# One of the weight sums of a Strassen product moves from VectorE to GpSimd

## The chip, the cores and the metric

The kernel runs on one core of one Trainium2 chip. The metric is the device time of one execution in microseconds (us). Before the change it is 801.15 us, the median of three runs (801.14, 801.15 and 801.73).

The core's engines are named as in its profile: PE is TensorE (matrix products; PEld is its load of the stationary operand, which overlaps the products), DVE is VectorE, ACT is ScalarE, POOL is GpSimd, and SP is the engine whose queue issues most DMAs. Every engine works through its own queue in order. "PEq", "SPq" and the like are the sequencers, which issue DMAs and carry out waits.

## The reference

One block of a decoder on 512 tokens of 1024 values, in float32: a mixer (a state-space part with 16 heads and a pooling part, with one input and one output projection), a cross-attention into 256 memory tokens, and a SwiGLU layer of width 2816. Each is preceded by an RMS norm and added to the residual. A last RMS norm gives the output. The change is in the SwiGLU layer alone:

```python
def swiglu(u, w_gate_up, w_down):
    gate, up = jnp.split(u @ w_gate_up, 2, axis=-1)
    return (jax.nn.silu(gate) * up) @ w_down

h = h + swiglu(rmsnorm(h, ffn_norm[l]), w_gate_up[l], w_down[l])
return rmsnorm(h, final_norm)
```

## The kernel before

**Precision.** Products run on TensorE in a rounded format (float32r). To reach float32 precision, every operand is split in two: `hi` is the operand rounded by ScalarE (a cast), `lo` is the remainder, operand minus `hi`, taken by VectorE. A product is then three matmuls: hi by hi, hi by lo, lo by hi. For activations the parts are called t_xh and t_xl (or t_xq where both lie in one tile), for weights `whi` and `wlo`. The cast of a weight tile is line 202, its remainder line 204; both handle 128 x 1024 elements, the unit in which weights are loaded.

**Seven products in place of eight.** The two matrix products of SwiGLU use Strassen's scheme in Winograd's form: operands are cut into 2 x 2 quadrants, and seven products of sums of quadrants replace eight products of quadrants. For the weights, with quadrants 11, 12, 21 and 22, the products are numbered by "form":

- forms 1, 2 and 4 are the quadrants 11, 12 and 22 themselves;
- form 5 is 21 + 22 and form 7 is 21 + 11;
- form 6 is form 5 + quadrant 11;
- form 3 is form 6 + quadrant 12.

The sums of the activations are made on chip by `forms` (lines 1126 to 1163), for one pair of activation tiles at a time: VectorE adds and subtracts (lines 1141, 1142, 1149, 1151), ScalarE casts (line 1132), and VectorE takes the remainders (line 1136).

**The stages.** The layer is cut into 17 chunks of weights: ten "g" chunks of 128 x 1024 (gate and up, blocks 0 to 4, two chunks each), one "g" chunk for block 5, and six "d" chunks (down, three blocks of two; the last of these is 512 wide). The order is a list written out by hand, SPEC: blocks g0 and g1, then d0, then g2 and g3, d1, g4 and g5, d2. Within a block the forms run in the order 1, 2, 5, 6, 3, 7, 4. In a d block, the products of forms 1, 2 and 5 are given in pieces, as the activations that they need come out of two turns (`i_turnff`, a transposition on TensorE, copies on ScalarE, and then `forms`) that stand beside the first of them. PSUM banks are named gA, gB, gC and dA, dB, dC after the output that they gather: forms 1, 6, 7 and 4 go to A, 5 and 3 to B, 2 to C. VectorE drains the banks (lines 1066, 1095 and 1211) and notes the last of these drains in `st["drained"]`.

**How the weight sums are made.** `load_strassen` (lines 147 to 173) loads quadrants by DMAs from SP's queue. For forms 5 and 7 it loads quadrant 21 and then adds the other quadrant by an accumulating DMA, which is issued from GpSimd's queue (line 171). `split_unit` (lines 182 to 211) is a generator of three steps, the sum if there is one, the cast and the remainder. When it has split form 2, it issues the sum for form 6 as another accumulating DMA from GpSimd's queue: form 5 is added onto the tile of quadrant 11 (line 210, "wq<-raw" in the profile). Only block g5 makes form 6 on VectorE (line 189). For form 3 it adds form 6 to the tile of quadrant 12, in place, on VectorE (line 193). The next step of the generator is the cast that reads the sum.

**What sets the order.** The program gives the order in which instructions are written; `advance` (end of the program) runs `split_unit` for the weights of the coming slot, and loads up to seven weight units ahead. A planner of the framework then places the instructions on each engine's queue by that priority and by its own estimate of when their operands are there. `after(later, earlier)` adds an edge which has no wait at run time, since both instructions are on one engine, and which makes the planner keep that order. The add of line 193 has such an edge behind the drain which was the latest when form 5 of the same chunk was split (lines 194, 195 and 201).

**Buffers.** There are six tiles for raw weights, two each for quadrants 11 and 12 of a chunk ("wq" in the profile), four for `whi`, five for `wlo`, and six PSUM banks for these products.

Of the kernel before, what the change touches and what calls it, by code (L numbers as in the profile page):

```python
# [10 lines left out]
ALU = mybir.AluOpType  # L11
# [49 lines left out]
def hybrid_block(ctx: ExitStack, tc: tile.TileContext, a: dict, out: bass.AP,  # L61
                 act_bufs=69, la=1, wb=(6, 4, 5), eng="", dact=(0, 1), raw_n=6, warm=12, spec=None, start=START, smm=START_MM, hu=1, dbg=None):
    nc = tc.nc
# [11 lines left out]
    def nm(base):  # L75
        uid[0] += 1
        return f"{base}_{uid[0]}"
# [69 lines left out]
    def load_strassen(key):  # L147

        _, c, f = key
        n = units[key][1]  # L150

        def quad(q):
            return a["w_s"][c, QUAD[q], :, :n]

        def plain(q, tag=None):
            if tag:
                t = act.tile([P, NC, 2, P], F32, tag=tag, name=nm("wq"), bufs=2).rearrange("p c q l -> p (c q l)")
            else:
                t = wraw.tile([P, 1024], F32, tag="raw", name=nm("raw"))
            nc.sync.dma_start(t[:, :n], quad(q))  # L160
            return t

        if f == 1:
            sw[c, 1] = plain("11", "m")
        elif f == 2:
            sw[c, 2] = plain("12", "m2")
        elif f == 4:
            sw[c, 4] = plain("22")
        elif f == 7 or f == 5 and (c, 5) not in sw:
            sw[c, f] = plain("21")  # L170
            nc.gpsimd.dma_start(sw[c, f][:, :n], quad("11" if f == 7 else "22"), accum_op=ALU.add)  # L171
        ready[key] = None
# [9 lines left out]
    def split_unit(key):  # L182
        n = units[key][1]
        raw = ready[key]
        if key[0] == "s":
            c, f = key[1:]
            if f == 6 and (c, 6) not in sw:
                sw[c, 6] = sw.pop((c, 1))
                nc.vector.tensor_tensor(out=sw[c, 6][:, :n], in0=sw[c, 6][:, :n], in1=sw[c, 5][:, :n], op=ALU.add)
                yield  # L190
            if f == 3:
                sw[c, 3] = sw.pop((c, 2))
                add = nc.vector.tensor_tensor(out=sw[c, 3][:, :n], in0=sw[c, 3][:, :n], in1=sw[c, 6][:, :n], op=ALU.add)  # L193
                if sw[c, "drained"] is not None:
                    after(add, sw[c, "drained"])
                yield
            raw = sw[c, f]
        hi = whi_p.tile([P, 1024], F32R, tag="hi", name=nm("whi"))
        lo = wlo_p.tile([P, 1024], F32R, tag="lo", name=nm("wlo"))
        if key[0] == "s" and f == 5:  # L200
            sw[c, "drained"] = st.get("drained")
        nc.scalar.copy(hi[:, :n], raw[:, :n])  # L202
        yield
        nc.vector.tensor_tensor(out=lo[:, :n], in0=raw[:, :n], in1=hi.bitcast(F32)[:, :n], op=ALU.subtract)  # L204
        ready[key] = (hi, lo)
        if key[0] == "s" and f == 2 and CHUNKS[c][:2] != ("g", 5):
            if (c, 5) not in sw:
                load_strassen(("s", c, 5))
            sw[c, 6] = sw.pop((c, 1))
            nc.gpsimd.dma_start(sw[c, 6][:, :n], sw[c, 5][:, :n], accum_op=ALU.add)  # L210
        yield

    def after(later, earlier):
        tc.add_manual_dep(later.ins, earlier.ins.name,
                          mybir.DependencyInfo(mybir.DependencyClass.NoSync, mybir.DependencyReason.DATA),
                          reason="order on one engine")
# [41 lines left out]
    sw = {}  # L258
# [79 lines left out]
    def i_start(its):  # L338
        it = Item(keys=["dt"] + [k for i in its[1:] for k in i.keys])

        def prep():
# [16 lines left out]
            for kind, i in [(t[0], int(t[1])) for t in start.split()]:  # L358
                if kind == "x":
                    st["xg"][i] = split("xg", xt[i], col(V_MIX + i))  # L360
                elif kind == "w":
                    drain(split_unit(it.keys[i]))
                elif kind in "hH":
                    n = units[it.keys[i]][1]
                    if kind == "h":
                        raws[i] = ready[it.keys[i]]
                        ready[it.keys[i]] = (whi_p.tile([P, 1024], F32R, tag="hi", name=nm("whi")),
                                             wlo_p.tile([P, 1024], F32R, tag="lo", name=nm("wlo")))
                    c = slice(0, n // 2) if kind == "h" else slice(n // 2, n)
                    hi, lo = ready[it.keys[i]]  # L370
                    split_into(hi[:, c], lo[:, c], raws[i][:, c])
                elif kind == "q":
                    sq_acc("xacc", xt[i])
                elif kind == "r":
                    drain(rms1.split())
                else:
                    drain(advance(i))
# [931 lines left out]
    def advance(t):  # L1309
        nonlocal lpos, spos  # L1310
        want = need_[min(t, len(slots) - 1)] - lead
        while spos < want:
            while lpos < min(spos + (7 if plan[spos][0] == "s" else wb[0] - 1), len(plan)):
                load_unit(plan[lpos])
                lpos += 1
            yield from split_unit(plan[spos])
            spos += 1
# [145 lines left out]
```

## Time and profile before

| | before |
|---|---|
| median of three runs | 801.15 us |
| profiled execution, its own time | 802.26 us |
| span of the profiled execution | 800.6 us |
| mean granted clock of TensorE | 0.994 |
| TensorE busy | 786.6 us, 98% |
| VectorE busy | 617.7 us, 77% |
| ScalarE busy | 487.5 us, 61% |
| GpSimd busy | 44.7 us, 6% |
| instructions | 10506 |

A row of a group names the line, the engine, the operation, "out<-in" by tiles, the shapes and the count; behind it stand the busy time, the mean duration of one in ns, and the idle time of the engine just before, with what ended it. A row of the waits is "who line <- what it waited for: us in total, times, longest us". A row of the timeline has the start, the duration (of all, where several are merged, "x2"), the engine, the line and the tiles, and in brackets the idle time before it with what ended that. A row of the windows has the stretch, its length, and for each engine the busy time and the count; then the granted clock of TensorE as a share of full speed, the share of the DMA engines, and GB/s. A row of the chain of waits has the start, the length and what the time went to. Instructions of one engine overlap a little: an instruction of 1.22 us on VectorE is followed by the next after 1.14.

### The profile page before, as it was taken

What the parts mean: (1) busy time and instruction counts of PE and PEld (TensorE: products, weight loads), DVE (VectorE), ACT (ScalarE), POOL (GpSimd) and SP (SyncE); (2) the same over time, 40 slices, a digit from 0 to 9 for tenths busy, and PEclk for the clock granted to TensorE, in tenths of its full rate; (3) what the DMA queues carried; (4) which work ended last, traced back from release to release, by engine and by line L of the source; (5) the groups of instructions that cost most, each with busy time, mean ns of one, the idle gap of its engine ahead of it and who ended that gap; (6) DMA issues with size and microseconds to landing.
All of it is one profiled execution on the core that took longest, in us unless ns stands there. A gap on an engine that the chain in (4) does not pass through costs nothing.

```text
span 800.6 us, 10506 instructions
## 1 busy us (share of the span) xinstructions
PE 786.6 (98%) x3856; PEld 662.1 (83%) x3856; DVE 617.7 (77%) x906; ACT 487.5 (61%) x777; POOL 44.7 (6%) x60
## 2 busy tenths in 40 slices
PE   9999999999999999999999999998999999999995
PEld 7878888888888889888888888887888887888984
DVE  7989969999884897346656667878766789767897
ACT  8667699567954456335544695755354666355864
POOL 0000000000000000000000001011111011101000
PEclk9999999999999999999999999999999999999998
DMA  8253425143574225322366278787779797879602
GB/s 329 89 171 106 130 75 178 53 129 102 185 262 142 86 99 179 111 79 80 114 149 158 54 158 229 188 239 155 214 176 266 178 249 164 227 166 269 160 15 105
DMA packets 40131, 124.42 MB, mean 155 GB/s; under 512 B 4736, under 2 KB 7168, under 8 KB 40080
## 3 DMA queue, kind: packets, MB, share of 16 engines
q1 hardware_dynamic: 32880, 98.33, 36.8%
q0 software_dynamic: 7200, 25.43, 17.7%
q8 instruction: 30, 0.49, 0.3%
q14 instruction: 21, 0.17, 0.1%
HBM read 113.48 MB, written 2.13 MB: 144 GB/s over the span
## 4 chain that ended last, share of the span: by engine, by line
PE 85%; DVE 7%; DMA 3%; ACT 3%; issue 2%; SPq 0%; ACTq 0%; DVEq 0%
PE gA L1054 13%; PE gB L1054 8%; PE dA L1054 6%; PE gC L1054 4%; PE dB L1054 3%; PE v L117 3%; PE v L118 3%; PE v L116 2%; DVE wlo L204 2%; PE wo L118 2%; PE op L118 2%; PE op L116 2%; PE wo L116 2%; PE q L117 2%; PE op L117 2%; PE q L116 2%
## 5 line engine op out<-in xcount | busy, mean ns | idle before, releaser
L202 ACT CAST whi<-raw 128x1024 fp32r<-128x1024 f32 (+1 forms) x127 | 131.4, 1040 | 131.1 <-issue 20.4
L204 DVE TENSOR_TENSOR wlo<-raw,whi 128x1024 fp32r<-128x1024 f32 (+1 forms) x127 | 152.3, 1208 | 61.3 <-ACT whi L202 60.7
L202 ACT CAST whi<-wq 128x1024 fp32r<-128x1024 f32 (+1 forms) x68 | 69.2, 1026 | 53.5 <-PE dA L1054 19.8
L204 DVE TENSOR_TENSOR wlo<-wq,whi 128x1024 fp32r<-128x1024 f32 (+1 forms) x68 | 80.4, 1189 | 25.8 <-ACT whi L202 25.6
L1054 PE MATMUL gA<-whi,t_xh 128*128 128x512 f32 (+1 forms) x192 | 71.7, 373 | 0.0
L1054 PE MATMUL gA<-wlo,t_xh 128*128 128x512 f32 (+1 forms) x192 | 71.4, 372 | 0.0
L1054 PE MATMUL gA<-whi,t_xl 128*128 128x512 f32 (+1 forms) x192 | 71.3, 371 | 0.0
L171 POOL DMA_DIRECT2D raw<-w_s x34 | 29.3, 862 | 655.0 <-DVE t_Pl L240 405.6
L1054 PEld LDWEIGHTS gA<-wlo,t_xh 128*128 128x128 f32 x192 | 36.1, 188 | 6.3
L1054 PEld LDWEIGHTS gA<-whi,t_xh 128*128 128x128 f32 x192 | 36.1, 188 | 6.3
L1054 PEld LDWEIGHTS gA<-whi,t_xl 128*128 128x128 f32 x192 | 36.2, 188 | 6.2
L1054 PE MATMUL dA<-whi,t_xl 128*128 128x512 f32 x88 | 34.5, 392 | 3.2 <-DVE t_xl L1136 3.2
L1054 PE MATMUL dA<-wlo,t_xh 128*128 128x512 f32 x88 | 34.3, 390 | 0.0
L1054 PE MATMUL dA<-whi,t_xh 128*128 128x512 f32 x88 | 34.0, 391 | 0.1
L1070 ACT ACTIVATE t_gu<-t_gu,s 128x512 f32<-128x512 f32 (+1 forms) x24 | 16.4, 687 | 27.9 <-DVE t_gu L1066 27.9
L193 DVE TENSOR_TENSOR wq<-wq,wq 128x1024 f32<-128x1024 f32 (+1 forms) x17 | 20.3, 1192 | 14.0 <-DMA wq<-raw 13.9
L1054 PE MATMUL gB<-whi,t_xq 128*128 128x512 f32 (+1 forms) x96 | 27.6, 371 | 0.0
L1132 ACT CAST t_xh<-t_x 128x512 fp32r<-128x512 f32 x30 | 18.6, 620 | 14.1 <-DVE t_x L1142 9.5
L116 PE MATMUL z<-t_uh,whi 128*128 128x512 f32 x64 | 25.2, 394 | 0.6 <-ACT t_uh L232 0.6
L116 PE MATMUL wo<-t_oh,whi 128*128 128x512 f32 x64 | 25.2, 394 | 0.0
L116 PE MATMUL v<-t_uh,whi 128*128 128x512 f32 x64 | 25.1, 392 | 0.0
L116 PE MATMUL q<-t_hgh,whi 128*128 128x512 f32 x64 | 25.1, 392 | 0.0
(382 smaller groups left out, 2237.8 us busy)
## 6 DMA issues: line engine op xcount, KB each, us to landing
raw<-w_u SPq DMA_DIRECT2D x76, 512.0 KB, 3.3
raw<-w_s SPq DMA_DIRECT2D x48, 512.0 KB, 4.3
wq<-w_s SPq DMA_DIRECT2D x32, 512.0 KB, 5.1
raw<-w_s POOLq DMA_DIRECT2D x32, 512.0 KB, 6.8
wq<-raw POOLq DMA_DIRECT2D x15, 512.0 KB, 7.4
t_x<-xT SPq DMA_DIRECT2D x16, 256.0 KB, 5.3
t_abc<-d_acs SPq DMA_DIRECT2D x16, 256.0 KB, 4.5
out<-t_hT SPq DMA_DIRECT2D x8, 256.0 KB, 2.3
```

The source lines that it names most:

```text
L116: nc.tensor.matmul(ps, whi, xhi, start=start, stop=False)
L117: nc.tensor.matmul(ps, whi, xlo, start=False, stop=False)
L118: nc.tensor.matmul(ps, wlo, xhi, start=False, stop=stop)
L171: nc.gpsimd.dma_start(sw[c, f][:, :n], quad("11" if f == 7 else "22"), accum_op=ALU.add)
L193: add = nc.vector.tensor_tensor(out=sw[c, 3][:, :n], in0=sw[c, 3][:, :n], in1=sw[c, 6][:, :n], op=ALU.add)
L202: nc.scalar.copy(hi[:, :n], raw[:, :n])
L204: nc.vector.tensor_tensor(out=lo[:, :n], in0=raw[:, :n], in1=hi.bitcast(F32)[:, :n], op=ALU.subtract)
L1054: nc.tensor.matmul(it.ps[tt], p[:, ts_], w[:, ws], start=first, stop=(c, i, n) == pairs[-1] and p is xh and w is wl, skip_group_check=True)
L1070: st["silu"] = nc.scalar.activation(g, g, AF.Silu, scale=st["r3",][:, c:c + 1])
L1132: nc.scalar.copy(h if w is None else h[:, w], src)
```

## The change

The add of form 3 is written to GpSimd in place of VectorE, with the same operands and in the same place of the program. The edge that kept it behind a drain of PSUM is not made any more; the note of that drain in line 201 stays, unused.

```diff
             if f == 3:
                 sw[c, 3] = sw.pop((c, 2))
-                add = nc.vector.tensor_tensor(out=sw[c, 3][:, :n], in0=sw[c, 3][:, :n], in1=sw[c, 6][:, :n], op=ALU.add)
-                if sw[c, "drained"] is not None:
-                    after(add, sw[c, "drained"])
+                nc.gpsimd.tensor_tensor(out=sw[c, 3][:, :n], in0=sw[c, 3][:, :n], in1=sw[c, 6][:, :n], op=ALU.add)
                 yield
```

There are 17 such adds, one for each chunk. The add of line 189 (form 6 of block g5) stays on VectorE.

## The prediction

> **What bounds the kernel now.** I read the page's busy table first, then who TensorE waits for in the stretch that holds the 17 adds (440 us to the end), then that stretch by windows, and last the chain of waits around the two holes found there.
>
> ```profile
> span 800.6 us, 10506 instructions
> PE 786.6 (98%) x3856; PEld 662.1 (83%) x3856; DVE 617.7 (77%) x906; ACT 487.5 (61%) x777; POOL 44.7 (6%) x60
> ```
> ```profile
> PE dA L1054 <- DVE t_xl L1136: 3.2, 2, 2.0
> ```
> ```profile
> core 0: us, PE busy (x) PEld busy (x) DVE busy (x) ACT busy (x) POOL busy (x), PEclk, DMA share, GB/s
> 552.70:554.80 2.10, 0.09 (x2) 0.07 (x1) 2.10 (x5) 0.62 (x1) 0.00 (x0) 1.00 0.69 217
> 555.80:559.30 3.50, 3.50 (x10) 2.73 (x9) 3.50 (x7) 2.46 (x3) 0.86 (x1) 0.51 0.75 179
> 674.00:676.00 2.00, 0.85 (x4) 0.41 (x3) 2.00 (x6) 0.62 (x1) 0.00 (x0) 1.00 1.02 277
> ```
>
> TensorE is busy 98% of the span, so work taken off VectorE is worth only what TensorE waits for VectorE. Behind the first 440 us that is two holes, 3.2 us in all, both before a dA product that waits for t_xl, a remainder which `forms` makes (L1136). The windows show them: 2.0 us at 552.7, and 1.15 us at 674.5. They also show what the longer one costs afterwards: from 555.8 the granted clock is 0.51 for 3.5 us, which loses 3.5 x 0.49 = 1.7 us. Behind the shorter one it stays at 1.00. So the two holes and the clock together are worth 2.01 + 1.15 + 1.7 = 4.9 us; the changed lines can take no more than that out of TensorE's time.
>
> The chain of waits through the first hole names its cause:
>
> ```profile
> 541.74 6.94 DMA wq<-raw
> ...
> 548.71 0.04 DVE wq L193
> ...
> 549.85 1.29 DVE t_xl L1136 x2
> 551.13 2.27 DVE wlo L204 x2
> ...
> 554.73 1.20 PE dA L1054 x4
> ```
>
> The accumulating DMA that makes form 6 of the second weight chunk lands at 548.7; the add of form 3 (L193), which needs it, stands in VectorE's queue ahead of the splits that TensorE is waiting for.
>
> **The change, part by part.** What it removes from VectorE, from the view of line 193 and from VectorE's waits between 440 and 775 us:
>
> ```profile
> L193 DVE TENSOR_TENSOR wq<-wq,wq x17: 684/1225/1227, 448.6 to 771.3; 128x1024 f32<-128x1024 f32 x16, 128x512 f32<-128x512 f32 x1
> ```
> ```profile
> DVE wq L193 <- DMA wq<-raw: 13.9, 11, 2.3
> ```
>
> That is 16 x 1.225 + 0.68 = 20.3 us of work and 13.9 us of waits for the DMA. Nearly all lies beside TensorE's work and is worth nothing. What counts is the two places. VectorE's timeline around the first, ScalarE's casts and TensorE's rows:
>
> ```profile
> 546.25 0.42 DVE L1151 SCALAR_TENSOR_TENSOR t_x<-t_x,t_fa 128x256 f32<-128x256 f32 x1
> 548.71 1.23 DVE L193 TENSOR_TENSOR wq<-wq,wq 128x1024 f32<-128x1024 f32 x1 [2.04 <-DMA wq<-raw]
> 549.85 1.29 DVE L1136 TENSOR_TENSOR t_xl<-t_x,t_xh 128x512 fp32r<-128x512 f32 x2
> 551.05 1.22 DVE L204 TENSOR_TENSOR wlo<-raw,whi 128x1024 fp32r<-128x1024 f32 x1
> 552.19 1.22 DVE L204 TENSOR_TENSOR wlo<-wq,whi 128x1024 fp32r<-128x1024 f32 x1
> 553.32 0.42 DVE L1141 TENSOR_TENSOR t_x<-t_fa,t_fb 128x256 f32<-128x256 f32 x1
> 553.66 0.42 DVE L1142 TENSOR_TENSOR t_x<-t_fb 128x256 f32<-128x256 f32 x1
> 553.99 0.69 DVE L1136 TENSOR_TENSOR t_xl<-t_fa,t_xh 128x512 fp32r<-128x512 f32 x1
> ```
> ```profile
> 546.70 0.62 ACT L1132 CAST t_xh<-t_x 128x512 fp32r<-128x512 f32 x1
> ...
> 548.68 1.06 ACT L202 CAST whi<-wq 128x1024 fp32r<-128x1024 f32 x1 [0.39 <-PE dB L1054]
> ```
> ```profile
> 552.34 0.39 PE L1054 MATMUL dB<-whi,t_xh 128*128 128x512 f32 x1
> 554.73 0.50 PE L1054 MATMUL dA<-whi,t_xl 128*128 128x512 f32 x1 [2.01 <-DVE t_xl L1136]
> ```
>
> Without the add, VectorE is free from 546.67. I walk its rows again with the waits that remain. The first t_xl ends at 547.2, the second may start when its cast ends (546.70 + 0.62 = 547.32) and takes 0.6, to 547.92. The next remainder takes 1.14, to 549.06. The one behind it waits for its own cast (548.68 + 1.06 = 549.74) and ends at 550.87. Then 0.34 + 0.33 + 0.69: the awaited t_xl is ready at 552.23, not 554.68. TensorE runs out of other work at 552.34 + 0.39 = 552.73. The hole closes with 0.5 us to spare, and with it goes the drop of the clock: 2.01 + 1.7 us.
>
> The second hole, the same way:
>
> ```profile
> 669.65 1.23 DVE L193 TENSOR_TENSOR wq<-wq,wq 128x1024 f32<-128x1024 f32 x1 [0.68 <-DMA wq<-raw]
> 670.79 1.29 DVE L1136 TENSOR_TENSOR t_xl<-t_x,t_xh 128x512 fp32r<-128x512 f32 x2
> ...
> 674.94 0.68 DVE L1136 TENSOR_TENSOR t_xl<-t_fa,t_xh 128x512 fp32r<-128x512 f32 x1
> ```
> ```profile
> 669.00 0.62 ACT L1132 CAST t_xh<-t_x 128x512 fp32r<-128x512 f32 x1
> ...
> 670.49 1.06 ACT L202 CAST whi<-wq 128x1024 fp32r<-128x1024 f32 x1
> ```
> ```profile
> 674.14 0.39 PE L1054 MATMUL dB<-whi,t_xh 128*128 128x512 f32 x1
> 675.68 0.50 PE L1054 MATMUL dA<-whi,t_xl 128*128 128x512 f32 x1 [1.15 <-DVE t_xl L1136]
> ```
>
> The second t_xl from 669.62 to 670.22, a remainder to 671.36, the next from its cast's end (671.55) to 672.68, the rest 1.36: ready at 674.04, and TensorE needs it at 674.53. Closed too, 1.15 us, again with 0.5 to spare.
>
> What it adds: 17 adds on GpSimd. The page has none there. From below, VectorE's own 1.23 us; from above, GpSimd's one elementwise kind with an input, below, scaled by the elements (8 x 0.29 = 2.3 us) and doubled for a second input, 4.6 us. I take 2.3, the row as it is.
>
> ```profile
> L108 POOL TENSOR_SCALAR_AFFINE_SELECT cmask<-cmask 128x128 f32<-128x128 f32 x1 | 0.3, 290 | 0.0
> ```
>
> GpSimd is 6% busy. Its queue is in order, and the other things in it are DMA issues; those around the first pair of adds, and the casts that read the two sums, are:
>
> ```profile
> 541.74 0.86 POOL L210 DMA_DIRECT2D wq<-raw  x1 [6.34 <-DVE wlo L204]
> 546.77 0.85 POOL L171 DMA_DIRECT2D raw<-w_s  x1 [4.16 <-DMA raw<-w_s]
> 556.25 0.86 POOL L171 DMA_DIRECT2D raw<-w_s  x1 [8.63 <-DVE t_x L1151]
> ```
> ```profile
> 557.22 1.04 ACT L202 CAST whi<-wq 128x1024 fp32r<-128x1024 f32 x1
> 560.77 1.05 ACT L202 CAST whi<-wq 128x1024 fp32r<-128x1024 f32 x1 [2.50 <-PE dB L1054]
> ```
> ```profile
> 566.24 0.61 PE L1054 MATMUL dB<-whi,t_xq 128*128 128x512 f32 x2
> ```
>
> The sums can start at about 542.6 and 548.7 and are read at 557.2 and 560.8, more than 12 us later; at 4.6 us each they are still in time, so their length costs nothing by itself. Queued behind a waiting add would be the issue at 546.77 (form 7): it slips by one add, and its weights are cast well after form 3's. Were both adds put behind the issue at 556.25, they would run from 557.1 to 561.7; ScalarE would wait some 2 us, and TensorE starts on form 3 at 566.24 only. Hidden as well. The order behind the PSUM sum that goes away concerns VectorE's queue alone and has no work of its own: nothing.
>
> What has no row is whether a VectorE instruction is held up while GpSimd reads the same memory. The add starts when its DMA lands, in the middle of the very splits that are late. From below it costs VectorE nothing. From above one add holds it for 2.3 us. If held for half of that, at the first hole: GpSimd from 549.06 to 550.2, remainder to 551.35, t_xl at 552.7, no hole; at the second: GpSimd from 670.22 to 671.37, two remainders to 673.65, t_xl at 675.0, a hole of 0.5. I take the half, as the ends are far apart and VectorE's rows follow one another so closely that a hold must fall on something.
>
> **Sum.** The profiled execution took 802.26 us for a span of 800.6; 2.01 + 1.15 + 1.7 go and 0.5 comes back: 802.26 - 4.4 = 797.9. The median of the runs is 1.1 below the profiled one: **796.8 us** (796.3 with no hold at all).
>
> **Rivals.** First, **full hold by the later add of a pair**. Hole one: GpSimd 549.06 to 551.4, remainder to 552.5, t_xl at 553.9, a hole of 1.15, which left the clock alone at 674; hole two: GpSimd 670.22 to 672.5, two remainders to 674.8, t_xl at 676.1, a hole of 1.6, 0.45 longer. 801.15 - 0.86 - 1.7 + 0.45 = 799.0, or 800.7 with one drop of the clock: about 799.9. For it: the rows stand back to back; against: VectorE waits for casts in both places, and these gaps take some of it.
>
> Second, **the side that gets slower**: both adds of a pair hold VectorE for their full length. The earlier one takes 2.3 where its own removal gave 1.14 (the spacing of 548.71 and 549.85), and pushes the end of the last form from 546.67 to 547.8. The first t_xl ends at 548.4, the second, behind its cast, at 549.1; the later add holds until 551.4; then 2.27 + 1.36 = 555.05, a hole of 2.3 in place of 2.0, and the clock drops as before. The second hole grows by the 0.45 above to 1.6, and the clock drops there too (1.7; the drop is decided somewhere between 1.15 and 2.0 us of idle time). 801.15 + 0.3 + 0.45 + 1.7 = 803.6. It decides once a pair's holds exceed the 2.45 us by which the t_xl of the first hole comes forward. The Trainium skill, page "SBUF — State Buffer", section "Who interferes with whom", speaks for this case: a VectorE instruction with two SBUF inputs and a GpSimd instruction that reads SBUF exclude each other, and the second one to issue is blocked until the first is done. No run here shows it so far; by that rule the time lies between the two rivals, without it at 796.3.
>
> Third, **the planner gives VectorE another order**: without the add and its order edge the splits of these blocks can be placed otherwise, so that one hole stays. With the first kept and the second gone: 801.15 - 1.15 = 800.0.
>
> **How the numbers follow.** Forecast 0.46 (own range 796.0 to 798.2), full hold of one add 0.22, of both 0.15, another order 0.17. No change means within 0.2%, 799.55 to 802.75, about what a measurement of this kernel can tell. Faster: 0.46, 0.09 of the first rival, 0.04 of the third: 0.59. Slower: 0.15 and 0.04 of the third: 0.19. Same: the rest, 0.22. The range for eight in ten reaches from below the free case over both neutral rivals: 795.8 to 802.4.
>
> **What would show it.** Right: no wait of dA for t_xl near 552 and 674, no granted clock of 0.51 behind it, line 193 on GpSimd at 2 to 3 us, VectorE's rows of 1.22 and 0.42 us unchanged beside it. Wrong: VectorE rows of the same shape that last 2 us and more while GpSimd adds, a cast of form 3 that waits for GpSimd, or new holes at the same products.

## The result, and the profile after

The changed kernel is slower: 804.74 us against 801.58 us for the kernel before on the same chips (medians of 17 runs each), a ratio of 1.0045 with a 95% interval of 1.0029 to 1.0061. Forecast were 796.8 us and a range up to 802.4. The profiled execution took 804.74 us, with a span of 803.0.

The change deletes two lines more than it adds, so line numbers behind it are smaller by two in this profile: the cast of a weight tile is L200, its remainder L202, the remainder t_xl L1134. The busy table of the page, and TensorE's waits behind 440 us:

```profile
span 803.0 us, 10545 instructions
PE 786.2 (98%) x3856; PEld 661.8 (82%) x3856; DVE 622.0 (77%) x889; ACT 486.8 (61%) x777; POOL 90.3 (11%) x77
```
```profile
PE dA L1052 <- DVE t_xl L1134: 4.1, 2, 2.4
PE ffT L1111 <- DVE t_gu L1093: 0.9, 1, 0.9
```

VectorE has lost 17 instructions and 20.3 us of adds, and yet it is busy for 622.0 us in place of 617.7. TensorE waits at the same two products as before, for 4.1 us in place of 3.2, and at a third place for 0.9. The groups of VectorE between 440 and 775 us (line, operation, tiles, count, busy time, mean of one in ns) show where the freed time went, first in the kernel before, then in the changed one:

```profile
L204 DVE TENSOR_TENSOR wlo<-wq,whi 128x1024 fp32r<-128x1024 f32 x63 | 76.6, 1221 | 25.8 <-ACT whi L202 25.6
L204 DVE TENSOR_TENSOR wlo<-raw,whi 128x1024 fp32r<-128x1024 f32 x46 | 55.5, 1221 | 17.4 <-ACT whi L202 16.9
L1136 DVE TENSOR_TENSOR t_xl<-t_x,t_xh 128x512 fp32r<-128x512 f32 x28 | 18.4, 684 | 0.2
```
```profile
L202 DVE TENSOR_TENSOR wlo<-wq,whi 128x1024 fp32r<-128x1024 f32 x62 | 81.4, 1318 | 28.2 <-ACT whi L200 28.0
L202 DVE TENSOR_TENSOR wlo<-raw,whi 128x1024 fp32r<-128x1024 f32 x46 | 67.3, 1475 | 28.4 <-ACT whi L200 27.7
L1134 DVE TENSOR_TENSOR t_xl<-t_x,t_xh 128x512 fp32r<-128x512 f32 x28 | 22.9, 845 | 0.2
...
L1140 DVE TENSOR_TENSOR t_x<-t_fb 128x256 f32<-128x256 f32 x13 | 7.2, 554 | 0.7 <-ACT t_fb L1011 0.7
L1064 DVE TENSOR_TENSOR t_gu<-t_gu,gB 128x512 f32<-128x512 f32 x10 | 6.8, 685 | 4.9 <-PE gB L1052 4.9
```

Instructions of the same shape with both inputs in SBUF last longer: 46 remainders by 0.254 us each (1.475 against 1.221), 62 by 0.097 (1.318 against the same 1.221), 28 t_xl by 0.161, 13 of the t_x by 0.135 (554 against 419 ns). That is 11.7 + 6.0 + 4.5 + 1.8 = 24 us, more than the 20.3 us that left. These means are carried by 14 rows, each at least 0.3 us longer than its like in the kernel before. The additions of a PSUM bank (L1064, one input in SBUF) stayed at 0.685 us, and the one at 590.74 ran wholly within two adds on GpSimd, which follow one another there until 593.08:

```profile
590.74 0.68 DVE L1064 TENSOR_TENSOR t_gu<-t_gu,gC 128x512 f32<-128x512 f32 x1
```
```profile
586.39 6.69 POOL L193 TENSOR_TENSOR wq<-wq,wq 128x1024 f32<-128x1024 f32 x2 [6.50 <-issue]
```

The 17 adds on GpSimd, from the page:

```profile
L193 POOL TENSOR_TENSOR wq<-wq,wq 128x1024 f32<-128x1024 f32 (+1 forms) x17 | 45.7, 2690 | 58.9 <-DVE wlo L202 41.7
```

The timelines of VectorE and of GpSimd around the first hole show two of the long rows and what ran beside them:

```profile
542.95 2.73 DVE L202 TENSOR_TENSOR wlo<-wq,whi 128x1024 fp32r<-128x1024 f32 x1 [1.05 <-ACT whi L200]
...
547.99 1.23 DVE L202 TENSOR_TENSOR wlo<-raw,whi 128x1024 fp32r<-128x1024 f32 x1
549.13 3.51 DVE L1134 TENSOR_TENSOR t_xl<-t_x,t_xh 128x512 fp32r<-128x512 f32 x2
552.56 1.21 DVE L202 TENSOR_TENSOR wlo<-wq,whi 128x1024 fp32r<-128x1024 f32 x1
...
554.37 0.68 DVE L1134 TENSOR_TENSOR t_xl<-t_fa,t_xh 128x512 fp32r<-128x512 f32 x1
```
```profile
542.20 2.39 POOL L193 TENSOR_TENSOR wq<-wq,wq 128x1024 f32<-128x1024 f32 x1 [5.74 <-DVE wlo L202]
544.55 0.86 POOL L208 DMA_DIRECT2D wq<-raw  x1
...
549.33 2.76 POOL L193 TENSOR_TENSOR wq<-wq,wq 128x1024 f32<-128x1024 f32 x1 [2.72 <-DVE wlo L202]
```

The first add runs from 542.20 to 544.59. The remainder issued at 542.95 ends at 545.68, which is 1.09 us behind the add's end: it stood still until GpSimd was done, and then ran at its usual length. At 549.13 it is the other way first: a t_xl is running when the second add is issued, the add comes behind it (2.76 us in place of 2.39), and the second t_xl waits for the add: two t_xl take 3.51 us where they took 1.29. The t_xl that TensorE needs is ready at 555.05, against 554.68 before. This execution runs 0.45 us later at that point (the drain of gA ahead of these rows starts at 540.02, before at 539.57), so the t_xl is about as late as it was, although the add has left VectorE's queue.

The second hole, in the same view of VectorE, and the windows around both holes (the columns are those explained above):

```profile
662.87 3.42 DVE L202 TENSOR_TENSOR wlo<-wq,whi 128x1024 fp32r<-128x1024 f32 x1 [1.05 <-ACT whi L200]
...
669.75 3.51 DVE L1134 TENSOR_TENSOR t_xl<-t_x,t_xh 128x512 fp32r<-128x512 f32 x2
```
```profile
553.00:555.50 2.50, 0.80 (x4) 0.35 (x3) 2.50 (x6) 0.62 (x1) 0.24 (x1) 1.00 0.47 170
673.00:676.00 3.00, 0.64 (x3) 0.28 (x2) 3.00 (x7) 0.62 (x1) 0.59 (x1) 1.00 0.48 173
677.10:680.50 3.40, 3.40 (x10) 2.65 (x9) 3.40 (x7) 2.12 (x3) 0.00 (x0) 0.51 0.98 158
```

TensorE now idles 2.50 - 0.80 = 1.70 us at the first hole (2.01 before) and 3.00 - 0.64 = 2.36 us at the second (1.15 before). The drop of the clock to 0.51 for 3.4 us has moved from the first hole to the second and costs the same 1.7 us. The third place is in the last d block, where an add at 764.2 holds a remainder for 3.31 us, and the activations behind it reach TensorE 0.93 us late:

```profile
764.36 3.31 DVE L202 TENSOR_TENSOR wlo<-raw,whi 128x1024 fp32r<-128x1024 f32 x1
```

Sum of what the stretch behind 440 us lost: 1.70 + 2.36 + 0.93 - 2.01 - 1.15 = 1.8 us of 2.4 us by which the span grew. Most of the rest is TensorE's first wait for data, at 7 us (1.1 us here, none before), which lies ahead of every changed instruction and differs from run to run.

### The profile page after: what moved, and what is told of

Its sections match the earlier page's. It is cut to its first block, busy times and chain, and to the rows that moved or that the text cites. A ratio compares the mean times of both kernels' runs of the same rounds, so it can differ in the third digit from the quotient of the medians.

```text
span 803.0 us, 10545 instructions
## 1 busy us (share of the span) xinstructions
PE 786.2 (98%) x3856; PEld 661.8 (82%) x3856; DVE 622.0 (77%) x889; ACT 486.8 (61%) x777; POOL 90.3 (11%) x77
## 4 chain that ended last, share of the span: by engine, by line
PE 86%; DVE 8%; ACT 3%; issue 1%; DMA 1%; SPq 0%; DVEq 0%
PE gA L1052 14%; PE gB L1052 7%; PE dA L1052 7%; PE gC L1052 4%; PE dB L1052 3%; PE v L117 2%; PE v L118 2%; PE v L116 2%; DVE wlo L202 2%; PE wo L118 2%; PE op L118 2%; PE op L116 2%; PE wo L116 2%; PE op L117 2%; PE q L117 2%; PE q L116 2%
## 5 line engine op out<-in xcount | busy, mean ns | idle before, releaser
L202 DVE TENSOR_TENSOR wlo<-raw,whi 128x1024 fp32r<-128x1024 f32 (+1 forms) x127 | 164.3, 1302 | 72.3 <-ACT whi L200 71.5
L200 ACT CAST whi<-raw 128x1024 fp32r<-128x1024 f32 (+1 forms) x127 | 131.3, 1040 | 132.2 <-issue 25.7
L202 DVE TENSOR_TENSOR wlo<-wq,whi 128x1024 fp32r<-128x1024 f32 (+1 forms) x68 | 86.4, 1278 | 28.2 <-ACT whi L200 28.0
L200 ACT CAST whi<-wq 128x1024 fp32r<-128x1024 f32 (+1 forms) x68 | 69.0, 1025 | 49.9 <-PE gA L1052 19.0
L193 POOL TENSOR_TENSOR wq<-wq,wq 128x1024 f32<-128x1024 f32 (+1 forms) x17 | 45.7, 2690 | 58.9 <-DVE wlo L202 41.7
```

The lines of the kernel that those rows point to most:

```text
L193: nc.gpsimd.tensor_tensor(out=sw[c, 3][:, :n], in0=sw[c, 3][:, :n], in1=sw[c, 6][:, :n], op=ALU.add)
```

## The experiments

The first theory, **hold**: an add on GpSimd stops a VectorE instruction with two SBUF inputs for as long as it runs, and in the d blocks that instruction is one that TensorE waits for. The rivals: **planner** (without the add, the planner gave VectorE and ScalarE another order in the d blocks, which it did: one weight remainder now stands ahead of the two t_xl, and in the profile above it is the row at 547.99), and **queue** (GpSimd's DMA issues now stand behind adds, as the one at 544.55, which stood at 541.74, so that sums come later). In all the kernels below, line numbers are those of the kernel before. Each diff is against the kernel before, where nothing else is said; a diff with added lines only puts them in place of the add and its edge.

### The add cut to one column

```diff
-                add = nc.vector.tensor_tensor(out=sw[c, 3][:, :n], in0=sw[c, 3][:, :n], in1=sw[c, 6][:, :n], op=ALU.add)
-                if sw[c, "drained"] is not None:
-                    after(add, sw[c, "drained"])
+                nc.gpsimd.tensor_tensor(out=sw[c, 3][:, :1], in0=sw[c, 3][:, :1], in1=sw[c, 6][:, :1], op=ALU.add)
```

> The changed kernel with the add cut to the first column of each tile (the other columns of form 3 stay without form 6, so that part of the sum is left out). The order on TensorE, VectorE, ScalarE and SP is that of the changed kernel; GpSimd is occupied for a fraction of a microsecond in place of 2.7. Theory hold (a GpSimd add that reads SBUF stops a VectorE instruction with two SBUF inputs for as long as it runs): no VectorE row is stretched, the waits of dA for t_xl go or fall under 0.5 us, about 796 to 797.5. Rival planner (the other order that the planner gave VectorE and ScalarE is what costs): the holes stay, 803 to 805. Rival queue (the DMA issues of GpSimd come later, behind the adds): as hold.

Measured: 797.25 us against 801.65, ratio 0.9949 (0.9936 to 0.9962). No wait of TensorE is left behind 440 us. The order of the instructions on TensorE, VectorE, ScalarE and SP is that of the changed kernel, and so is the place of the adds in GpSimd's queue; so the other order costs nothing, and the planner rival falls. No row of VectorE behind 440 us is longer than its like in the kernel before by more than 0.06 us. The groups:

```profile
L204 DVE TENSOR_TENSOR wlo<-raw,whi 128x1024 fp32r<-128x1024 f32 x46 | 55.9, 1223 | 29.6 <-ACT whi L202 28.4
```
```profile
L193 POOL TENSOR_TENSOR wq<-wq,wq 128x1 f32<-128x1 f32 x17 | 7.8, 460 | 66.1 <-DVE wlo L204 32.8 <-issue 23.0 <-DMA wq<-raw 5.1
```

### GpSimd as long at work, but only writing

```diff
+                nc.gpsimd.tensor_tensor(out=sw[c, 3][:, :1], in0=sw[c, 3][:, :1], in1=sw[c, 6][:, :1], op=ALU.add)
+                for _ in range(2):
+                    nc.gpsimd.memset(sw[c, 3][:, :n], 1.0)
```

> As the one-column kernel, but behind each one-column add GpSimd fills the tile of form 3 twice, so it is occupied for about 2.1 us per sum and writes the same tile without reading it (form 3 is left out of the weights here). Theory hold by reading: VectorE's remainders stay at 1.22 us, 796 to 798. If GpSimd's writing alone holds VectorE, or if GpSimd's occupied queue is what costs (later DMA issues, later sums): remainders of 2 to 3.5 us or holes as in the changed kernel, 803 to 805.

Measured: 797.74 us against 801.65, ratio 0.9950 (0.9937 to 0.9962). GpSimd is busy for 0.43 + 2 x 0.93 us per sum, its DMA issues wait behind that, and VectorE's remainders stay at 1.223 us, again with no row that is longer by more than 0.06 us:

```profile
L195 POOL MEMSET wq<- 128x1024 f32 (+1 forms) x34 | 31.7, 931 | 2.0
```
```profile
L204 DVE TENSOR_TENSOR wlo<-raw,whi 128x1024 fp32r<-128x1024 f32 x46 | 55.9, 1223 | 29.7 <-ACT whi L202 28.5
```

So it is neither GpSimd's time nor its queue; what the add has and the fills lack is that it reads SBUF (a GpSimd instruction with one input was not tried). The queue rival falls with it.

### Half of the columns

```diff
+                nc.gpsimd.tensor_tensor(out=sw[c, 3][:, :n // 2], in0=sw[c, 3][:, :n // 2], in1=sw[c, 6][:, :n // 2], op=ALU.add)
```

> The changed kernel with the add cut to the first half of the columns (the second half of form 3 stays without form 6, so that part of the sum is left out); the order on TensorE, VectorE, ScalarE and SP is that of the changed kernel. GpSimd's add then takes about 1.3 us in place of 2.4 to 2.8. Theory hold: VectorE rows are stretched by at most 1.2 us, each pair's hold is about what the freed place gives, and the holes at dA go or stay under 0.5 us: 797 to 799. If an add of any length costs the whole hole (the order of the two engines decides, not the time): 803 to 805.

Measured: 797.37 us against 801.29, ratio 0.9953 (0.9938 to 0.9968), and no wait of TensorE behind 440 us. The adds take 1.6 us on average (the shortest took 1.28):

```profile
L193 POOL TENSOR_TENSOR wq<-wq,wq 128x512 f32<-128x512 f32 (+1 forms) x17 | 27.1, 1597 | 60.6 <-DVE wlo L204 36.5 <-issue 14.4 <-DMA wq<-raw 5.2
```

With shorter holds the t_xl are in time. In this run the remainder and the two t_xl of the first hole last 1.59 and 2.39 us, so the pair of adds holds VectorE for 0.4 + 1.1 = 1.5 us; in the changed kernel the same rows give 1.5 + 2.2 = 3.7 us. The cost is not proportional to the hold: 1.5 us cost nothing and 3.7 us cost a hole. The prediction put the limit for a pair at 2.45 us, which lies between the two.

### Each add in two halves

```diff
+                for h_ in (slice(0, n // 2), slice(n // 2, n)):
+                    nc.gpsimd.tensor_tensor(out=sw[c, 3][:, h_], in0=sw[c, 3][:, h_], in1=sw[c, 6][:, h_], op=ALU.add)
```

> The changed kernel with each add cut into two instructions of half the columns, one behind the other; all sums are complete. If VectorE gets in between two GpSimd instructions, no row of it is stretched by more than about 1.3 us; the sum of the holds stays: 800 to 804. If GpSimd's next instruction follows without letting VectorE in, as the two adds did that held one remainder for 4.24 us in the kernel with late adds: single rows of 3.3 us and more as in the changed kernel, 803 to 806.

Measured: 803.97 us against 801.29, ratio 1.0030 (1.0015 to 1.0045), with holes at dA of 2.20 and 1.55 us. VectorE's and GpSimd's timelines at the first:

```profile
551.74 1.51 DVE L1141 TENSOR_TENSOR t_x<-t_fa,t_fb 128x256 f32<-128x256 f32 x1
553.18 1.48 DVE L1142 TENSOR_TENSOR t_x<-t_fb 128x256 f32<-128x256 f32 x1
```
```profile
550.74 3.63 POOL L194 TENSOR_TENSOR wq<-wq,wq 128x512 f32<-128x512 f32 x2 [3.27 <-DVE t_xl L1136]
```

Here the engines took turns: two instructions of 0.42 us were held for 1.1 us each. No single row is held for the length of both. With the remainder at 542.66 (1.96 us for 1.22) and the row at 544.55 (1.50 us for 0.42), the holds of this pair add up to 4.0 us, against 3.7 in the changed kernel, and the intervals of the two times overlap. Cutting each add in two did not take the loss away.

### The d chunks alone, and the g chunks alone

The first kernel puts the adds of the six d chunks on GpSimd and leaves the eleven of the g chunks on VectorE with their edge; the second does the reverse ("g" for "d" in both lines).

```diff
-                add = nc.vector.tensor_tensor(out=sw[c, 3][:, :n], in0=sw[c, 3][:, :n], in1=sw[c, 6][:, :n], op=ALU.add)
-                if sw[c, "drained"] is not None:
+                add = (nc.gpsimd if CHUNKS[c][0] == "d" else nc.vector).tensor_tensor(out=sw[c, 3][:, :n], in0=sw[c, 3][:, :n], in1=sw[c, 6][:, :n], op=ALU.add)
+                if CHUNKS[c][0] != "d" and sw[c, "drained"] is not None:
```

> Half of the change: the adds of the six d chunks on GpSimd, those of the eleven g chunks on VectorE with their edge as before. Theory hold, decided in the d blocks alone: all of the loss, 803 to 806. If holds in the g blocks carry the loss: 800 to 802.

> The other half of the change: the adds of the eleven g chunks on GpSimd, those of the d chunks on VectorE with their edge. The d chunks alone gave 804.9 with two larger holes, so theory hold says that the g blocks have slack for it: VectorE rows are stretched there, no new wait on TensorE, 801 to 802.5 as before. If holds in the g blocks cost as well: 803 or more.

Measured: d alone 804.87 us against 801.65, ratio 1.0029 (1.0012 to 1.0046); g alone 801.83 us against 800.99, ratio 1.0013 (0.9994 to 1.0032), not told apart from no change. TensorE's waits behind 440 us, of d alone and of g alone:

```profile
PE dA L1054 <- DVE t_xl L1136: 4.7, 2, 2.5
PE ffT L1113 <- DVE t_gu L1095: 0.9, 1, 0.9
```
```profile
PE dA L1054 <- DVE t_xl L1136: 2.5, 2, 1.2
```

The d chunks carry the loss, all three places of it. With the g chunks on GpSimd, VectorE's raw remainders are as long as in the changed kernel (1.503 us on average), and TensorE waits no longer than before: so what VectorE splits there is needed later.

### The adds of the d chunks later, on GpSimd

Against the changed kernel; `st["L1", x, i]` keeps the first remainder that `forms` makes.

```diff
+                add, late = nc.gpsimd.tensor_tensor(...), st.get(("L1", "ff", 4 * CHUNKS[c][1] + 3)) if CHUNKS[c][0] == "d" else None
+                if late is not None:
+                    tc.add_manual_dep(add.ins, late.ins.name, ...)
...
-        rest(L1, FA, H1)
+        st["L1", x, i] = rest(L1, FA, H1)
```

> The changed kernel, with the adds of the d chunks kept back until the first remainder of the block's last turn (the t_xl that dA waits for) is done. The order on TensorE, VectorE, ScalarE and SP is that of the changed kernel. Theory hold: the add still stretches VectorE rows, but later ones, on which nothing waits; the two holes go, 796.5 to 799. Rival planner: the holes stay, 803 to 805. Rival queue: GpSimd's adds are as long as before and come later still, no better than 803.

Measured: 811.28 us against 801.65, ratio 1.0110 (1.0084 to 1.0137): a miss, far on the wrong side. The profile is of the fastest of the six executions (805.81 us; the others took 808.83 to 813.72, at a lower granted clock of TensorE), so it shows where the loss lies, but not all of it. The t_xl came in time, as meant: the two waits for it are gone. The hold only moved. Timelines of VectorE and GpSimd, and TensorE's waits:

```profile
557.42 4.24 DVE L204 TENSOR_TENSOR wlo<-wq,whi 128x1024 fp32r<-128x1024 f32 x1
```
```profile
554.95 0.86 POOL L171 DMA_DIRECT2D raw<-w_s  x1 [6.93 <-DVE t_hT L1211]
555.51 5.05 POOL L193 TENSOR_TENSOR wq<-wq,wq 128x1024 f32<-128x1024 f32 x2
```
```profile
PE dA L1054 <- DVE wlo L204: 5.3, 2, 2.8
PE ffT L1113 <- DVE t_gu L1095: 0.9, 1, 0.9
```

Both adds of the pair now stand behind a DMA issue that waits until 554.95, and follow one another. The weight remainder of form 6, issued at 557.42, stood still until both were over (560.56) and took 4.24 us; TensorE waited for it instead. I had assumed that nothing waits on the VectorE rows behind the t_xl; the remainder of form 6 was as urgent. In this kernel VectorE did not get in between two adds, in the one with halves it did; why, these runs do not show.

### The adds of the d chunks later, on VectorE

```diff
-                add = nc.vector.tensor_tensor(...)
-                if sw[c, "drained"] is not None:
-                    after(add, sw[c, "drained"])
+                add, late = nc.vector.tensor_tensor(...), st.get(("L1", "ff", 4 * CHUNKS[c][1] + 3)) if CHUNKS[c][0] == "d" else None
+                if late is not None or sw[c, "drained"] is not None:
+                    after(add, late if late is not None else sw[c, "drained"])
...
-        rest(L1, FA, H1)
+        st["L1", x, i] = rest(L1, FA, H1)
```

> The kernel before, with the adds on VectorE, but those of the first two d blocks ordered behind the first remainder of the block's last turn (the t_xl that dA waits for). If what the kernel before loses in its two holes is the place of the add in VectorE's queue, both holes go without any help from GpSimd: 796.5 to 798.5. If VectorE's work itself is too much there, the holes move to a later remainder: 799 to 802.

Measured: 798.55 us against 800.99, ratio 0.9969 (0.9956 to 0.9981): faster than both kernels, with all sums complete. No wait of TensorE is left behind 440 us. VectorE's timeline:

```profile
551.55 0.69 DVE L1136 TENSOR_TENSOR t_xl<-t_fa,t_xh 128x512 fp32r<-128x512 f32 x1
...
559.34 2.35 DVE L193 TENSOR_TENSOR wq<-wq,wq 128x1024 f32<-128x1024 f32 x2
```

The awaited t_xl is ready at 552.24, and the two adds run as a pair at 559.34, behind the remainder of form 6. What the kernel before loses was the place of the add in VectorE's queue, and the same queue has a place for it, without another engine. No run here found such a place on GpSimd.

### A third DMA in place of the add

```diff
+                nc.gpsimd.dma_start(sw[c, 3][:, :n], sw[c, 6][:, :n], accum_op=ALU.add)
```

> Form 3 is summed by an accumulating DMA from GpSimd's queue, as form 6 is, so neither VectorE nor GpSimd reads the tiles. Theory hold: no stretched VectorE row and no add in VectorE's queue, the two holes go as with the one-column add: 796.5 to 798.5, if each sum lands (some 7 us after form 6) before its cast. If the second DMA comes too late, ScalarE's casts wait for it and TensorE for the remainders: 799 to 803. If the gain of the one-column kernel came from having no sum to make rather than from the engines' freedom: no better than 801.

Measured: 801.37 us against 800.99, ratio 0.9997 (0.9982 to 1.0013): no change. The two holes at t_xl are gone here too, but ScalarE waits for sums that land late. A sum of block g5, issued at 735.51, lands 7.2 us later; the casts and remainders behind it are late up to the last d block, where TensorE waits (ScalarE's waits, then TensorE's):

```profile
ACT whi L202 <- DMA wq<-wq: 20.1, 5, 6.3
```
```profile
PE dA L1054 <- ACT whi L202: 1.9, 1, 1.9
PE dA L1054 <- DVE wlo L204: 0.7, 1, 0.7
PE dB L1054 <- DVE wlo L204: 0.3, 1, 0.3
```

The time alone would fit a last rival, that the one-column kernel gained by having no sum to make. The kernel with late adds on VectorE refutes it: it makes all sums and took 798.55 us.

### The edge alone

```diff
-                add = nc.vector.tensor_tensor(...)
-                if sw[c, "drained"] is not None:
-                    after(add, sw[c, "drained"])
+                nc.vector.tensor_tensor(...)
```

> The edge alone: the adds on VectorE without the order behind a PSUM drain. The planner moves three of the adds a little earlier on VectorE, one in each of the first two d blocks among them, two places ahead, where it waits for the DMA. Theory hold gives the edge no part in the loss: 801 to 803. If taking the edge away costs by itself: 803 to 806, with a longer hole at dA and VectorE waiting for the DMA ahead of it.

Measured: 808.17 us against 800.99, ratio 1.0092 (1.0070 to 1.0114): the edge is worth 7 us on VectorE, more than either expectation. The profile is of the slowest of the six executions (812.28 us). Three adds move up, and two of these matter. VectorE's timeline and TensorE's waits:

```profile
543.15 1.23 DVE L193 TENSOR_TENSOR wq<-wq,wq 128x1024 f32<-128x1024 f32 x1 [4.99 <-DMA wq<-raw]
544.30 1.22 DVE L204 TENSOR_TENSOR wlo<-raw,whi 128x1024 fp32r<-128x1024 f32 x1
545.43 0.74 DVE L1095 SCALAR_TENSOR_TENSOR t_gu<-gA,s,t_gu 128x512 f32<-128x512 f32 x1
```
```profile
PE ffT L1113 <- DVE t_gu L1095: 8.6, 2, 5.4
```

The add now waits 5 us for its DMA ahead of L1095, the drain that the edge had kept in front of it, and whose output TensorE must transpose next. So the two halves of the change are not independent: on GpSimd the edge has nothing to protect, and on VectorE it must stay.

## Why the prediction was wrong

**What bounds the kernel** was right. The two holes, the clock behind the longer one and the add in VectorE's queue as their cause are shown: the kernel with one column differs from the changed one in the width of the add alone, has neither hole and took 797.25 us (the prediction's free case was 796.3), and late adds on VectorE close both holes too. Its walk through the first hole (awaited t_xl at 552.23) was met to 0.01 us by the kernel with late adds on VectorE, in another order of the rows between.

**The step that failed** is the hold, and in it the sentence "I take the half, as the ends are far apart". The trace had no row for it, and the two ends were 0 and 2.3 us. The walk charged 1.15 us for the later add of each pair and nothing for the earlier one, without a reason. Measured were 1.5 us for the first add of the first hole (2.73 against 1.22) and 2.2 for the second (3.51 against 1.29), and 2.2 us for each of the second hole: 3.7 and 4.4 us for a pair, where the forecast had 1.15. That the kernel with half the columns took 797.37 us, near the 796.8 forecast, is in part luck: it has no hole where the forecast left one of 0.5 us, and the forecast is too low by what follows.

**From the profile to the median.** The sum takes the 1.7 us of the clock out of the profiled execution (802.26 us, mean granted clock 0.994), and then another 1.1, as the median lies lower. But that execution is longer than the median mostly through this very drop: beside the experiments, 14 executions of the kernel before at a clock of 0.994 took 803.2 us on average, and 30 at 0.997 or 0.998 took 800.8. So the 1.1 us is in the main counted twice. Without it the free case is 802.26 - 4.9 = 797.4, and one column measured 797.25.

**The length of the add** was predicted as 2.3 us; the shortest row of 128 x 1024 is 2.39. The mean of 2.69 includes GpSimd's own waiting for VectorE.

**The rivals.** The second, both adds holding VectorE for their full length, is what happened. It had a chance of 0.15 and a time of 803.6; its t_xl at 555.05 was measured at 555.05, by way of a different order of the rows and in an execution that runs 0.45 us later, so that the agreement to the last digit is luck. Its two holes of 2.3 and 1.6 us were 1.7 and 2.4; the clock dropped once and not twice, in the profiled execution; and the third place, in the last d block, was not in it. The Trainium skill, page "SBUF — State Buffer", section "Who interferes with whom", which spoke for this rival, agrees with the runs: the rows with two SBUF inputs are held (up to 3.4 us for 1.22), those with one input in PSUM are not (0.685 us), and a GpSimd instruction that only writes holds nothing (1.223 us beside 0.93 us fills). The rule was at hand, it named the very pair of instructions, and the argument for taking the half came from no row; the chance should have lain with the rule.

**GpSimd's queue** was taken to be harmless, and that holds: the later DMA issue (544.55 for 541.74) and the sums that come later are hidden, as the kernel with fills shows.

**The planner** did give VectorE another order, as the third rival said, and it cost nothing: the same order gave 797.25 us with one column.

**The order edge** was costed at nothing "as it concerns VectorE's queue alone". For this change that is right; the edge alone shows that it is worth 7 us as long as the add is on VectorE.

**The spread.** The changed kernel's runs spread from 801.6 to 809.5 us, those of the kernel before from 799.5 to 803.4. Most of this goes with TensorE's clock: of the 17 executions, the seven at a mean granted clock of 0.997 or 0.998 took 801.62 to 804.13 us, the four at 0.992 or 0.993 took 806.14 to 809.53. One drop of 3.4 us to half is 0.002 of the mean. The seven average 802.8 us, 2.0 more than the 30 of the kernel before at the same clocks, which agrees with the 1.8 us of idle time above; the rest of the 3.2 us between the medians goes with the clock. Which holes are followed by a drop in the executions without a trace is not shown.

## What to carry to other kernels

An add that moves to GpSimd is not off VectorE's path if it reads SBUF while VectorE does: each engine waits for the other's whole instruction, and the time comes back on whichever VectorE instruction of that kind is next, here the splits that TensorE waits for, since the adds become ready among them. Before moving an instruction to another engine because it waits in the wrong place of a queue, look for a better place in the same queue: one order edge gave 0.3% here, while the other engine cost 0.45%. Where a shared resource has no row in the trace, price it in full if a rule names it, and let the slack of each place decide, as holds of 1.5 us in a pair cost nothing here, and those of 3.7 us cost more than the add's removal gave.

## What the runs showed of the hardware

Holds go both ways and last to the end of the other's instruction: a GpSimd add of 2.39 us lasted up to 3.38 where VectorE came first, and a VectorE remainder of 1.22 up to 3.42. Two adds in a row made one remainder last 4.24 us in one kernel, while in another a short VectorE instruction got in between two half adds. A GpSimd add of one column takes 0.46 us on average. TensorE's clock dropped for 3.4 us behind idle times of 2.01, 2.36 and 1.9 us and not behind 1.15, 1.70 and 2.20, so the length of the idle time alone does not decide it.

The clock records of the traces hint at what does. Every stretch at full clock in the twelve traces lasts a whole number of periods of 3.413 us, counted from the first rise of the clock (161 periods in the kernel before, 197 and then 34 in the changed one). With these periods laid over TensorE's rows, a period at full clock with 1.67 us of idle time or more was followed by one at half clock, and one with 1.57 us or less was not; the one exception, 1.79 us without a drop, lies at the end of the run with the d chunks alone. The 2.01 us of the kernel before fall into one period. The 1.70 us of the changed kernel are split into 0.89 and 0.81, and the 2.20 us of the kernel with halves into 0.90 and 1.30. So where a hole falls in these periods decides as well as its length. This is read from twelve executions; no run was made to test it.
